# A fused decoder layer on one Trainium2 core: the head's conditioning matmuls set between the transposes of x, first tokens on VectorE, first weight splits at fixed places

## The chip, the cores and the metric

One Trainium2 chip, one of its cores. A core has five engines with instruction queues of their own: TensorE (PE; its weight loads are shown apart as PEld), VectorE (DVE), ScalarE (ACT), GpSimd (POOL) and SyncE (SP, which only issues DMAs here). Sixteen DMA engines are shared by all queues that issue DMAs. The metric is the device time of one execution in microseconds (us); a lower number is better. It covers the program's span and what lies around it.

## The reference

One layer of a hybrid decoder for 256 prompt tokens and 8 x 8 sample tokens (320 columns together), all in float32. What the head of the kernel has to do is the first three lines:

```
mod = silu(c) @ w_ada + b_ada;  sh1, sc1, g1, sh2, sc2, g2 = split(mod, 6)
h = rmsnorm(x, norm1_g) * (1 + sc1) + sh1
p = h @ w_in                      # q, k, v, og, u, ga, gb, alr
o, s_new = gla(q, k, v, decay(alr));  y_a = rmsnorm(o) * silu(og);  y_b = pool(u)
x = x + g1 * ((sigmoid(ga) * y_a + sigmoid(gb) * y_b) @ w_o)
gate, up = split((rmsnorm(x) * (1 + sc2) + sh2) @ w_gu, 2)
y = rmsnorm(x + g2 * ((silu(gate) * up) @ w_down))
```

D_MODEL is 2048 (16 tiles of 128, counted by k), w_in has 11280 columns, w_ada 12288, the FFN 5632.

## The kernel before

Activations stand transposed: 128 features on the partitions, 320 tokens in the free dimension. A projection multiplies in three passes (`mm3`, lines 166 to 168) with both operands split into a high and a low part: of the weights `whi` and `wlo` (ScalarE casts, line 152; VectorE subtracts, line 153), of the tokens `hh` and `hl`. Every weight chunk is loaded by SyncE in program order into the tile `raw`, of which the pool holds three (`bufs=3`); a fourth load waits until the oldest has been split. Tiles `whi` and `wlo` have five buffers each (`WB`).

The head makes the first tokens. It loads c and x, transposes c, makes `scT` = silu(c), and transposes x: 16 tiles, each by three transposes (128, 128 and 64 rows, by `tr`, line 129) into PSUM (`misc`, four buffers) and a copy into `xT` by ScalarE and VectorE in turn (line 458). ScalarE sums the squares of x (line 472); square root, reciprocal and three matmuls with a diagonal matrix `dg` (line 480) give `rx`, the inverse norms, on every partition. `HeadJob` multiplies `scT` with the first two feature tiles' columns of w_ada: four `burst`s of 32 instructions (`ada_mm`, line 218), each on two loads `raw` of w_ada of 512 KB (tag `araw`, eight buffers), then `finish`: a copy `adasb`, a transpose, and `mod` on VectorE (lines 232, 235). `h_unit(k)` makes `hh[k]` and `hl[k]` from `xT[k]`, `rx` and `mod`, on VectorE, GpSimd (64 sample columns) and ScalarE.

Then a loop over slices of k, (0, 2), (2, 4), (4, 8), (8, 12), (12, 16), makes the early projections of each slice and adds them up in SBUF: q, k, v, u, og, ga, gb of the first head and gb of two others. With two feature tiles in a slice, v, og, ga and gb come from one load of 512 columns (`proj_pair`), q, k and u from 256 columns (`proj`). Between these, the bursts and `h_unit`s of the next slice are set; `spill` writes `xT` to DRAM (`xspill`) by GpSimd's queue. Behind the slices follow the other heads' projections, w_o, w_gu and w_down, all in the same manner.

The order on each engine is laid out when the program is built: a scheduler may move an instruction up or down its engine's list, except among those marked by `keep_in_program_order`, which keep theirs (all loads of the slices, and the first matmul of each group in `ada_mm`).

Of the kernel before, what the change touches and what calls it, by code (L numbers as in the profile page):

```python
# [11 lines left out]
F32 = mybir.dt.float32  # L12
F32R = mybir.dt.float32r
I32 = mybir.dt.int32
AF = mybir.ActivationFunctionType
ALU = mybir.AluOpType
# [4 lines left out]
P = 128  # L21
TP, NB, LS = 256, 8, 8
TS = NB * LS
T = TP + TS
D = 2048
KT = D // P
# [10 lines left out]
WB = 5  # L37
AB = 3
SLICES = ((0, 2), (2, 4), (4, 8), (8, 12), (12, 16))
# [41 lines left out]
def body(tc, A):  # L81
    nc = tc.nc
    ctx = ExitStack()
    cp = ctx.enter_context(tc.tile_pool(name="cp", bufs=1))
    wp = ctx.enter_context(tc.tile_pool(name="wp", bufs=3))
# [3 lines left out]
    hp = hcx.enter_context(tc.tile_pool(name="hp", bufs=1, side="right"))  # L89
# [7 lines left out]
    def nm(s):  # L97
        uid[0] += 1
        return "%s_%d" % (s, uid[0])

    def misc():
        return pmisc.tile([P, 512], F32, tag="m", name=nm("pm"))
# [32 lines left out]
    def raw_chunk(src, nk, nn, pool=None, tag="raw", bufs=3):  # L135

        if pool is None and more:
            more.reverse()
            if more[0] is not None:
                pool, bufs = more[0], 2  # L140
        t = (pool or wp).tile([P, nk, nn], F32, tag=tag, bufs=bufs, name=nm("raw"))
        ins = nc.sync.dma_start(t, src)
        if in_order[0]:
            tc.keep_in_program_order(ins)
        return t
# [7 lines left out]
        V.tensor_sub(lo, raw, hi.bitcast(F32))  # L153
        return hi, lo

    def split_chunk(src, nk, nn):

        raw = raw_chunk(src, nk, nn)
        step = 512 // nn
        for k in range(0, nk, step):  # L160
            hi, lo = split(raw[:, k:min(k + step, nk)])
            for j in range(hi.shape[1]):
                yield k + j, hi[:, j], lo[:, j]
# [6 lines left out]
    def proj(w, col, k0, k1, xh, xl):  # L170

        ps = pmain.tile([P, 2, 512], F32, tag="pm", name=nm("ps"))
        for c0 in range(k0, k1, 4):
            nk = min(4, k1 - c0)
            for j, whi, wlo in split_chunk(w[:, c0:c0 + nk, col:col + 256], nk, 256):
                kt = c0 + j
                for i in range(2):
                    mm3(ps[:, i, :T], whi[:, i * P:(i + 1) * P], wlo[:, i * P:(i + 1) * P],
                        xh[kt], xl[kt], kt == k0, kt == k1 - 1)
            ada_pump()  # L180
        return ps
# [14 lines left out]

    def proj_pair(w, col, k0, k1, xh, xl):

        parts = list(split_chunk(w[:, k0:k1, col:col + 512], k1 - k0, 512))
        for half in range(2):  # L200
            ps = pmain.tile([P, 2, 512], F32, tag="pm", name=nm("ps"))
            for j, whi, wlo in parts:
                kt = k0 + j
                for i in range(2):
                    c = (2 * half + i) * P
                    mm3(ps[:, i, :T], whi[:, c:c + P], wlo[:, c:c + P], xh[kt], xl[kt], kt == k0, kt == k1 - 1)
            yield ps
# [78 lines left out]
    def modp(sec, kt):  # L286
        return mod[:, sec * KT + kt, 0:1]

    def mods(sec, kt):
        return mod[:, sec * KT + kt, 1:9].unsqueeze(2).broadcast_to([P, NB, LS])  # L290

    def s3(ap):
        return ap.rearrange("p (b t) -> p b t", t=LS)

    hh = [hp.tile([P, T], F32R, tag="hh%d" % k, name="hh%d" % k) for k in range(KT)]
    hl = [None] * KT
# [70 lines left out]
    def units(h):  # L367
        return [("q", 0, OQ + DK * h), ("k", 0, OK_ + DK * h), ("v", 0, OV + DV * h),
                ("v", 1, OV + DV * h + 256), ("u", 0, OU + 256 * h),
                ("og", 0, OOG + DV * h), ("og", 1, OOG + DV * h + 256),  # L370
                ("ga", 0, OGA + DV * h), ("ga", 1, OGA + DV * h + 256),
                ("gb", 0, OGB + DV * h), ("gb", 1, OGB + DV * h + 256)]


    with tc.tile_pool(name="head", bufs=1) as xp:
# [2 lines left out]
        nc.sync.dma_start(crow[0:1, :], A["c_prompt"])  # L378
        nc.sync.dma_start(crow[1:9, :], A["c_sample"])
        xn = [xp.tile([P, D], F32, name="xn%d" % i) for i in range(3)]  # L380
        x2d = A["x_prompt"][0]
        nc.sync.dma_start(xn[0], x2d[0:P])
        nc.sync.dma_start(xn[1], x2d[P:2 * P])
        nc.sync.dma_start(xn[2][0:TS], A["x_sample"].rearrange("b t d -> (b t) d"))
        V.memset(scT, 0.0)
        make_identity(nc, ident)
        vr0 = xp.tile([6 * KT, P], F32, name="vr0")
# [17 lines left out]
        class HeadJob:  # L405


            def __init__(self, b0, s):
                self.b0, self.s, self.w, self.nk = b0, s, 64 * s, 8 // s
                self.ps = None  # L410
                self.raws = {}
# [34 lines left out]


        xT = []
        for k in range(KT):
            pt = misc()  # L450
            for i in range(3):
                n = P if i < 2 else TS
                tr(pt[:, i * P:i * P + n], xn[i][:n, k * P:(k + 1) * P])
            if k < SLICES[0][1]:
                xT.append(xp.tile([P, T], F32, name="xT%d" % k))
            else:
                xT.append(hp.tile([P, T], F32, tag="hl%d" % k, name="xT%d" % k))
            (S.copy if k % 2 else V.tensor_copy)(xT[k], pt[:, 0:T])

        pt = misc()  # L460
        tr(pt[:, 0:96], vr0)
        tr(pt[:, 96:164], vr1)
# [2 lines left out]
        for sec in (1, 4):  # L465
            V.tensor_scalar(bada[:, sec * KT:(sec + 1) * KT], bada[:, sec * KT:(sec + 1) * KT], 1.0, None, op0=ALU.add)

        ssq = xp.tile([P, 3], F32, name="ssq")
        V.memset(ssq, 1.0)
        for i in range(3):  # L470
            n = P if i < 2 else TS
            S.activation(junk[:n], xn[i][:n], AF.Square, accum_out=ssq[:n, i:i + 1])
        S.activation(ssq, ssq, AF.Sqrt, scale=1.0 / D, bias=epst)
        V.reciprocal(ssq, ssq)
        prs = misc()
# [4 lines left out]
            PE.matmul(prs[:, i * P:i * P + n], lhsT=ones[:n, :], rhs=dg[:n, i, :n], start=True, stop=True)  # L480
        rx = xp.tile([P, T], F32, name="rx")
        V.tensor_copy(rx, prs[:, 0:T])

        def h_unit(k):
            t = xp.tile([P, T], F32, tag="xh", bufs=2, name=nm("xh"))
            V.scalar_tensor_tensor(t[:, 0:TP], xT[k][:, 0:TP], modp(1, k), rx[:, 0:TP], op0=ALU.mult, op1=ALU.mult)
            G.tensor_tensor(t[:, TP:T], xT[k][:, TP:T], rx[:, TP:T], op=ALU.mult)
            G.tensor_tensor(s3(t[:, TP:T]), s3(t[:, TP:T]), mods(1, k), op=ALU.mult)
            G.tensor_tensor(s3(t[:, TP:T]), s3(t[:, TP:T]), mods(0, k), op=ALU.add)
            S.activation(hh[k][:, 0:TP], t[:, 0:TP], AF.Identity, bias=modp(0, k))  # L490
            S.copy(hh[k][:, TP:T], t[:, TP:T])
            hl[k] = hp.tile([P, T], F32R, tag="hl%d" % k, name="hl%d" % k)
            V.scalar_tensor_tensor(hl[k][:, 0:TP], t[:, 0:TP], modp(0, k), hh[k][:, 0:TP].bitcast(F32),
                                   op0=ALU.add, op1=ALU.subtract)
            V.tensor_sub(hl[k][:, TP:T], t[:, TP:T], hh[k][:, TP:T].bitcast(F32))  # L495
# [25 lines left out]
        for h in EARLY_GB:  # L521
            ge = G0()
            ge.gb = merged[h]
            early += [(ge, "gb", i, OGB + DV * h + 256 * i) for i in range(2)]
        for f in HeadJob(0, SLICES[0][1]).steps():
            f()
        for k in range(SLICES[0][1]):
            h_unit(k)
        for si, (k0, k1) in enumerate(SLICES):
            bg = []  # L530
            acc = 0 if si == 0 else 1
# [604 lines left out]
```

## Time and profile before

| what | value |
|---|---|
| median of 3 runs | 2013.61 us (2013.16 to 2013.98) |
| profiled execution, its own time | 2011.32 us |
| span of that execution, first to last instruction | 2009.5 us |
| PE busy | 1956.2 us, 97% of the span |
| VectorE, ScalarE, GpSimd busy | 51%, 41%, 7% |
| mean granted TensorE clock | 0.989 |

Busy shares are of the whole span. The span is shorter than the execution's own time by 1.8 us that lie around it. The profile's times are counted from the first instruction of the program. A PE row's duration is a matmul's latency; matmuls overlap, so the distance between starts is what one costs.

### The profile page before, as it was taken

How to read it: one execution, taken by the hardware profiler on the slowest of the kernel's cores; microseconds unless marked ns; L12 is line 12 of the kernel's file. 1: busy time of each engine (PE TensorE's matmuls, PEld its weight loads, DVE VectorE, ACT ScalarE, POOL GpSimd, SP SyncE). 2: the span in 40 equal slices, each digit the busy share in tenths (PEclk: the TensorE clock that was granted, in tenths of full speed). 3: DMA queues.
4: the chain of work that ended last, by engine and by line, in shares of the span. 5: the costliest groups of instructions: out<-in, count | busy, mean ns of one | idle time of the engine just before them, and what ended most of it. 6: DMA issues, size and time to landing. Idle time of an engine off the chain costs nothing.

```text
span 2009.5 us, 37187 instructions
## 1 busy us (share of the span) xinstructions
PE 1956.2 (97%) x15008; PEld 1848.8 (92%) x15008; DVE 1015.5 (51%) x1881; ACT 820.1 (41%) x1466; POOL 141.8 (7%) x261
## 2 busy tenths in 40 slices
PE   7999999999999999999989999999999999999997
PEld 5789998888899899889979999999999999999997
DVE  3555665465546433665574444444444444444554
ACT  4333374354336333643344333343333344344443
POOL 1112220111001100110020000000000000000000
PEclk9999999999999999999989999999999999999998
DMA  9888754775975887569737666544444544444442
GB/s 301 285 302 272 234 155 147 253 255 186 314 237 167 281 263 229 156 230 340 234 105 223 206 205 203 168 148 154 145 152 149 155 149 147 151 154 144 150 142 91
DMA packets 319598, 400.83 MB, mean 199 GB/s; under 512 B 13529, under 2 KB 259801, under 8 KB 319089
## 3 DMA queue, kind: packets, MB, share of 16 engines
q1 hardware_dynamic: 307154, 358.21, 55.8%
q0 software_dynamic: 12272, 40.25, 5.7%
q8 instruction: 117, 1.92, 0.4%
q14 instruction: 55, 0.45, 0.1%
HBM read 373.96 MB, written 24.67 MB: 198 GB/s over the span
## 4 chain that ended last, share of the span: by engine, by line
PE 91%; DMA 5%; DVE 1%; ACT 1%; issue 1%; SPq 0%; POOL 0%; ACTq 0%; POOLq 0%; DVEq 0%
PE ps L166 27%; PE ps L168 26%; PE ps L167 26%; PE pm L218 5%; DMA raw<-w_in 2%; DMA raw<-w_ada 2%; PE pm L129 2%; PE pm L800 1%; PE pm L769 1%; PE pm L821 1%; DMA xn<-x_sample 1%; DVE wlo L153 0%; PE pm L796 0%; PE pm L758 0%; PE pm L641 0%
## 5 line engine op out<-in xcount | busy, mean ns | idle before, releaser
L153 DVE TENSOR_TENSOR wlo<-raw,whi 128x512 fp32r<-128x512 f32 x952 | 659.6, 697 | 834.0 <-ACT whi L152 827.2
L152 ACT CAST whi<-raw 128x512 fp32r<-128x512 f32 x952 | 587.0, 621 | 1013.4 <-PE ps L167 878.0
L166 PE MATMUL ps<-hh,whi 128*128 128x320 f32 x1408 | 445.9, 317 | 7.3 <-ACT whi L152 3.1
L166 PE MATMUL ps<-h2h,whi 128*128 128x320 f32 x1408 | 437.8, 311 | 5.1 <-ACT h2h L1042 5.1
L168 PE MATMUL ps<-hh,wlo 128*128 128x320 f32 x1408 | 441.6, 314 | 0.2 <-DVE wlo L153 0.2
L167 PE MATMUL ps<-hl,whi 128*128 128x320 f32 x1408 | 440.3, 313 | 0.3 <-DVE hl L495 0.3
L167 PE MATMUL ps<-h2l,whi 128*128 128x320 f32 x1408 | 435.5, 309 | 0.0
L168 PE MATMUL ps<-h2h,wlo 128*128 128x320 f32 x1408 | 435.5, 309 | 0.0
L166 PEld LDWEIGHTS ps<-hh,whi 128*128 128x128 f32 x1408 | 266.6, 189 | 30.8 <-issue 15.8
L168 PEld LDWEIGHTS ps<-hh,wlo 128*128 128x128 f32 x1408 | 266.6, 189 | 8.1 <-issue 6.1
L166 PEld LDWEIGHTS ps<-h2h,whi 128*128 128x128 f32 x1408 | 265.0, 188 | 9.3 <-ACT h2h L1042 6.1
L167 PEld LDWEIGHTS ps<-hl,whi 128*128 128x128 f32 x1408 | 266.9, 190 | 7.0 <-issue 5.4
L167 PEld LDWEIGHTS ps<-h2l,whi 128*128 128x128 f32 x1408 | 264.9, 188 | 0.0
L168 PEld LDWEIGHTS ps<-h2h,wlo 128*128 128x128 f32 x1408 | 264.9, 188 | 0.0
L166 PE MATMUL ps<-ah,whi 128*128 128x320 f32 x704 | 218.7, 311 | 0.0
L168 PE MATMUL ps<-ah,wlo 128*128 128x320 f32 x704 | 217.5, 309 | 0.0
L167 PE MATMUL ps<-al,whi 128*128 128x320 f32 x704 | 217.5, 309 | 0.0
L167 PEld LDWEIGHTS ps<-al,whi 128*128 128x128 f32 x704 | 132.2, 188 | 0.0
L166 PEld LDWEIGHTS ps<-ah,whi 128*128 128x128 f32 x704 | 132.2, 188 | 0.0
L168 PEld LDWEIGHTS ps<-ah,wlo 128*128 128x128 f32 x704 | 132.2, 188 | 0.0
L218 PE MATMUL pm<-raw,scT 128*32 128x128 f32 (+1 forms) x2688 | 109.9, 295 | 8.1 <-DMA raw<-w_ada 8.0
L218 PEld LDWEIGHTS pm<-raw,scT 128*32 128x32 f32 x2688 | 69.1, 111 | 36.0 <-issue 19.5
(279 smaller groups left out, 1542.6 us busy)
## 6 DMA issues: line engine op xcount, KB each, us to landing
raw<-w_ada SPq DMA_DIRECT2D x192, 512.0 KB, 5.8
raw<-w_gu SPq DMA_DIRECT2D x176, 512.0 KB, 3.5
raw<-w_in SPq DMA_DIRECT2D x173, 512.0 KB, 3.9
raw<-w_down SPq DMA_DIRECT2D x80, 512.0 KB, 3.3
S<-state_gla POOLq DMA_DIRECT2D x16, 1024.0 KB, 8.2
o_gs<-S POOLq DMA_DIRECT2D x16, 1024.0 KB, 5.9
raw<-w_o SPq DMA_DIRECT2D x32, 512.0 KB, 4.7
raw<-w_down SPq DMA_DIRECT2D x16, 256.0 KB, 2.6
```

The source lines that it names most:

```text
L129: PE.transpose(out, in_, ident[:k, :k])
L152: S.copy(hi, raw)
L153: V.tensor_sub(lo, raw, hi.bitcast(F32))
L166: PE.matmul(ps, lhsT=whi, rhs=xhi, start=start, stop=False)
L167: PE.matmul(ps, lhsT=whi, rhs=xlo, start=False, stop=False)
L168: PE.matmul(ps, lhsT=wlo, rhs=xhi, start=False, stop=stop)
L218: ins = PE.matmul(ps[32 * j:32 * j + 32, 0:w], lhsT=scT[:, k, :], rhs=raws[j], start=k == 0, stop=k == KT - 1, tile_position=(0, 32 * j))
L769: PE.matmul(pt, lhsT=E["kdn"][:, s, d * P:(d + 1) * P], rhs=E["vn"][:, s], start=s == 0, stop=s == 1)
L800: PE.matmul(pt[32 * j:32 * j + 32, :], lhsT=qeP[:, d, 4 * gg + j, :], rhs=E["S0", gg, d][:, j], start=False, stop=d == 1, tile_position=(0 ...
L821: PE.matmul(pt, lhsT=kpz[:, gg, j, d * P:(d + 1) * P], rhs=E["vp"][:, gg], start=True, stop=True)
```

## The change

Six edits, all in the head:

- The load of the sample rows of x (`xn[2]`) goes from SyncE's queue to ScalarE's, ahead of ScalarE's other work.
- The sum of squares stands ahead of the transposes. Only tiles 0 and 1 of x are transposed at first (copied by VectorE); the rest are made by a function `x_trans`, three tiles after each of the four bursts, and the last four after `finish`'s copy.
- The loads of w_ada of the first job and the first four loads of w_in (q, k, v, u) are issued ahead of everything that needs them.
- `x * rx` of the first two tiles is made early (`xhat`). `h_first` replaces `h_unit` for them and takes GpSimd's share to VectorE.
- The splits of q, k, v and u are five `EarlySplit`s, whose casts and subtractions are marked to keep the order in which the code names them; `split_chunk` hands them out from `ready`.
- `job0` is the `HeadJob` of the first slice, called step by step.

```diff
+        def hi(self):
+            tc.keep_in_program_order(S.copy(self.h, self.raw))
+        def lo(self):
+            tc.keep_in_program_order(V.tensor_sub(self.l, self.raw, self.h.bitcast(F32)))
...
+        nc.scalar.dma_start(xn[2][0:TS], A["x_sample"].rearrange("b t d -> (b t) d"))
...
-        nc.sync.dma_start(xn[2][0:TS], A["x_sample"].rearrange("b t d -> (b t) d"))
...
+        for i in range(3):
+            n = P if i < 2 else TS
+            S.activation(junk[:n], xn[i][:n], AF.Square, accum_out=ssq[:n, i:i + 1])
+        for k in range(SLICES[0][1]):
+            x_trans(k, 0)
...
+        for k in range(SLICES[0][1]):
+            t = xp.tile([P, T], F32, tag="xh", bufs=2, name=nm("xh"))
+            V.tensor_tensor(t, xT[k], rx, op=ALU.mult)
+            xhat.append(t)
+
+        def h_first(k):
+
+            t = xhat[k]
+            S.activation(hh[k][:, 0:TP], t[:, 0:TP], AF.Identity, scale=modp(1, k), bias=modp(0, k))
+            V.tensor_tensor(s3(t[:, TP:T]), s3(t[:, TP:T]), mods(1, k), op=ALU.mult)
+            V.tensor_tensor(s3(t[:, TP:T]), s3(t[:, TP:T]), mods(0, k), op=ALU.add)
+            S.copy(hh[k][:, TP:T], t[:, TP:T])
+            hl[k] = hp.tile([P, T], F32R, tag="hl%d" % k, name="hl%d" % k)
+            V.tensor_scalar(t[:, 0:TP], t[:, 0:TP], modp(1, k), modp(0, k), op0=ALU.mult, op1=ALU.add)
+            V.tensor_sub(hl[k], t, hh[k].bitcast(F32))
...
-        for f in HeadJob(0, SLICES[0][1]).steps():
-            f()
-        for k in range(SLICES[0][1]):
-            h_unit(k)
+        nx = SLICES[0][1]
+        for i, k0 in enumerate(range(0, KT, 4)):
+            job0.burst(k0)
+            while len(xT) < min(nx + 3 * (i + 1), KT - 4):
+                x_trans(len(xT), len(xT) % 2)
+        ew = []
+        for kind, i, col in units(0)[:5]:
+            if kind == "v" and i == 1:
+                continue
+            raw = raw_chunk(win[:, 0:nx, col:col + (512 if kind == "v" else 256)], nx, 512 if kind == "v" else 256)
+            ready[col] = [EarlySplit(raw)] if kind != "v" else [EarlySplit(raw[:, j:j + 1]) for j in range(nx)]
+            ew += ready[col]
+        ew[0].hi()
+        job0.finish()
+        h_first(0)
+        ew[0].lo()
+        ew[1].hi()
+        h_first(1)
+        while len(xT) < KT:
+            x_trans(len(xT), 1)
+        for e in ew[1:]:
+            if e is not ew[1]:
+                e.hi()
+            e.lo()
```

What the scheduler makes of it, at three places. TensorE, where the `rx` matmuls (lines 480 before, 510 after) stand; `pm` on `xn` are transposes of x, `pm` on `raw` is a burst. Before:

```order
L129 MATMUL pm_249<-cst,xn_120 128x128
L129 MATMUL pm_249<-cst,xn_121 128x128
L129 MATMUL pm_249<-cst,xn_122 128x64
L129 MATMUL pm_255<-cst,vr_131 128x96
L480 MATMUL pm_269<-dg,cst 128x128 x2
L480 MATMUL pm_269<-dg,cst 128x64
L218 MATMUL pm_296<-raw_284,scT 32x128 x2
```

After:

```order
L129 MATMUL pm_186<-cst,xn_121 128x128
L129 MATMUL pm_186<-cst,xn_122 128x64
L510 MATMUL pm_201<-dg,cst 128x128 x2
L510 MATMUL pm_201<-dg,cst 128x64
L242 MATMUL pm_220<-raw_159,scT 32x128 x2
```

The `rx` matmuls and all bursts stood behind all 16 tiles of x (`pm_249` is the last of them); now the `rx` matmuls stand behind two tiles (`pm_180`, `pm_186`) and ahead of the first burst, and the other 14 tiles stand behind them.

SyncE, from the last loads of w_ada of the first job on, with what each waits for (DMAHW names are earlier DMAs, PE and DVE the engine that frees a buffer). Before:

```order
L142 DMA raw_436<-w_in 128x2x512 [waits DMAHW7_49]
L142 DMA raw_474<-w_ada 128x4x256 [waits DMAHW0_49,PE_49]
L142 DMA raw_476<-w_ada 128x4x256 [waits DMAHW1_49,PE_49]
L142 DMA raw_479<-w_in 128x2x256 [waits DMAHW5_49,DMAHW2_49,DVE_49]
L142 DMA raw_500<-w_ada 128x4x256 [waits DMAHW3_49,PE_49]
```

After:

```order
L142 DMA raw_345<-w_in 128x2x256 [waits DMAHW5_49]
L142 DMA raw_349<-w_in 128x2x256 [waits DMAHW6_49]
L142 DMA raw_353<-w_in 128x2x512 [waits DMAHW7_49]
L142 DMA raw_359<-w_in 128x2x256 [waits DMAHW0_49,DMAHW5_49,DVE_49,Activation_49]
L142 DMA raw_478<-w_ada 128x4x256 [waits DMAHW1_49,PE_49]
L142 DMA raw_480<-w_ada 128x4x256 [waits DMAHW2_49,PE_49]
```

The load of u (`raw_479`, now `raw_359`), which takes over q's buffer, stood behind two loads of w_ada; now all six loads of w_ada for the next slice stand behind it.

ScalarE, from the copy `adasb` of `finish` to the first tokens (lines 490 and 491 before, 523 and 526 after). Before:

```order
L434 COPY adasb_365<-pm_296 128x128
L152 CAST whi_438<-raw_436 128x512
L152 CAST whi_442<-raw_436 128x512
L490 ACTIVATE hh_90<-xh_372,mod 128x256
L491 CAST hh_90<-xh_372 128x64
```

After:

```order
L458 COPY adasb_364<-pm_220 128x128
L483 COPY xT_343<-pm_339 128x320
L168 CAST whi_347<-raw_345 128x512
L483 COPY xT_391<-pm_387 128x320
L483 COPY xT_397<-pm_393 128x320
L523 ACTIVATE hh_90<-xh_211,mod 128x256
L523 ACTIVATE hh_91<-xh_213,mod 128x256
L483 COPY xT_403<-pm_399 128x320
L483 COPY xT_409<-pm_405 128x320
L526 CAST hh_90<-xh_211 128x64
```

Between `adasb` and the last piece of `hh_90` stood two casts and one activation; now eight instructions, five of them copies of transposed tiles. On VectorE the first subtraction of the weights (`wlo_348`, of q) stands behind `hl` of tile 0; before, it stood ahead of `mod`. From the og projection on, the order is the same on every engine.

## Rows read from the trace of the kernel before

**Rows 1.** The page's chain that ended last, by engine.

```profile
PE 91%; DMA 5%; DVE 1%; ACT 1%; issue 1%; SPq 0%; POOL 0%; ACTq 0%; POOLq 0%; DVEq 0%
```

**Rows 2.** Chain that ended last, 24 to 60 us: start us, us, what.

```profile
31.26 0.28 ACT adasb L434
...
33.55 11.29 DMA raw<-w_in
44.92 0.63 ACT whi L152
...
47.14 0.38 PE ps L166
```

**Rows 3.** PE in order of time: start us, us, operation, count, [idle <-releaser].

```profile
13.44 11.05 PE L129 MATMUL pm<-cst,xn 128*128 128x128 f32 x36 [0.27 <-DVE xT L458]
...
24.63 1.73 PE L480 MATMUL pm<-dg,cst 128*128 128x128 f32 x6
...
29.65 1.52 PE L218 MATMUL pm<-raw,scT 128*32 128x128 f32 x48
31.58 0.33 PE L129 MATMUL pm<-cst,adasb 128*128 128x128 f32 x1 [0.41 <-ACT adasb L434]
34.58 0.68 PE L166 MATMUL ps<-hh,whi 128*128 128x320 f32 x2 [2.68 <-ACT hh L491]
```

**Rows 4.** Stretches: length, busy us (instructions) PE, PEld, DVE, ACT, POOL, clock, DMA, GB/s.

```profile
9.00:12.40 3.40, 1.12 (x4) 0.72 (x4) 0.00 (x0) 2.00 (x2) 0.00 (x0) 1.00 0.95 205
13.00:25.00 12.00, 11.73 (x41) 6.18 (x40) 4.45 (x12) 6.24 (x13) 0.00 (x0) 1.00 1.10 353
...
26.00:28.00 2.00, 2.00 (x35) 1.75 (x38) 0.49 (x1) 0.14 (x1) 0.32 (x1) 1.00 0.07 23
...
26.29:27.99 1.70, 1.70 (x33) 1.58 (x36) 0.49 (x1) 0.00 (x0) 0.32 (x1) 1.00 0.03 10
...
34.90:38.20 3.30, 3.04 (x12) 2.67 (x11) 1.80 (x5) 0.82 (x3) 2.93 (x7) 0.50 1.00 325
38.30:39.90 1.60, 1.60 (x12) 1.60 (x12) 0.00 (x0) 0.34 (x1) 0.00 (x0) 1.00 1.00 304
...
47.00:80.00 33.00, 32.86 (x313) 29.93 (x317) 18.73 (x35) 12.34 (x23) 5.11 (x10) 1.00 0.82 273
```

**Rows 5.** ScalarE in order of time.

```profile
10.18 1.91 ACT L472 ACTIVATE junk<-xn 128x2048 f32<-128x2048 f32 x1 [1.19 <-DMA xn<-x_prompt]
11.99 0.19 ACT L472 ACTIVATION_READ_ACCUMULATOR junk<-xn 128x1 f32 x1
...
15.82 1.28 ACT L473 ACT_TABLE_LOAD   x1
...
22.69 0.43 ACT L458 COPY xT<-pm 128x320 f32<-128x320 f32 x1 [1.40 <-PE pm L129]
...
32.97 0.51 ACT L490 ACTIVATE hh<-xh,mod 128x256 fp32r<-128x256 f32 x1 [0.41 <-DVE xh L486]
34.28 0.24 ACT L491 CAST hh<-xh 128x64 fp32r<-128x64 f32 x1 [0.81 <-POOL xh L489]
```

**Rows 6.** VectorE in order of time.

```profile
17.74 0.64 DVE L479 TENSOR_SCALAR dg<-cst,ssq 128x128 f32<-128x128 f32 x3
...
32.24 0.18 DVE L235 TENSOR_TENSOR mod<-mod,vec 128x18 f32<-128x18 f32 x1
```

**Rows 7.** SyncE's issues in order of time.

```profile
28.24 0.92 SPq L142 DMA_DIRECT2D raw<-w_ada  x2
30.93 0.37 SPq L142 DMA_DIRECT2D raw<-w_in  x1
```

**Rows 8.** DMA issues of 30.93 to 31.30 us: KB each, median us to landing.

```profile
raw<-w_in SPq DMA_DIRECT2D x1, 256.0 KB, 3.2
```

**Rows 9.** PE in order of time, 328 to 333 us.

```profile
328.80 1.14 PE L129 MATMUL pm<-cst,w 128*128 128x128 f32 x9
```

**Rows 10.** PE's waits over the span: us in total, times, longest us.

```profile
PE ps L166 <- ACT whi L152: 3.1, 2, 1.8
```

More of the change, by code (lines that the diff above doesn't have):

```diff
@@ L154, in split, with __init__, split_chunk @@
         return hi, lo
-    def split_chunk(src, nk, nn):
+    ready = {}
+    class EarlySplit:
+        def __init__(self, raw):
+            n = raw.shape[2]
+            self.raw = raw
+            self.h = wp.tile([P, 512 // n, n], F32R, tag="whi", bufs=WB, name=nm("whi"))
+            self.l = wp.tile([P, 512 // n, n], F32R, tag="wlo", bufs=WB, name=nm("wlo"))
+        def hi(self):
+            tc.keep_in_program_order(S.copy(self.h, self.raw))
+        def lo(self):
+            tc.keep_in_program_order(V.tensor_sub(self.l, self.raw, self.h.bitcast(F32)))
+    def split_chunk(src, nk, nn, key=None):
+        if key in ready:
+            k = 0
+            for e in ready.pop(key):
+                for j in range(e.h.shape[1]):
+                    yield k, e.h[:, j], e.l[:, j]
+                    k += 1
+            return
         raw = raw_chunk(src, nk, nn)
@@ L174, in proj @@
             nk = min(4, k1 - c0)
-            for j, whi, wlo in split_chunk(w[:, c0:c0 + nk, col:col + 256], nk, 256):
+            for j, whi, wlo in split_chunk(w[:, c0:c0 + nk, col:col + 256], nk, 256, col if w is win else None):
                 kt = c0 + j
@@ L197, in proj_pair @@
     def proj_pair(w, col, k0, k1, xh, xl):
-        parts = list(split_chunk(w[:, k0:k1, col:col + 512], k1 - k0, 512))
+        parts = list(split_chunk(w[:, k0:k1, col:col + 512], k1 - k0, 512, col))
         for half in range(2):
@@ L448, in body, with x_trans @@
         xT = []
-        for k in range(KT):
+        def x_trans(k, eng):
             pt = misc()
@@ L457, in body @@
                 xT.append(hp.tile([P, T], F32, tag="hl%d" % k, name="xT%d" % k))
-            (S.copy if k % 2 else V.tensor_copy)(xT[k], pt[:, 0:T])
+            (S.copy if eng else V.tensor_copy)(xT[k], pt[:, 0:T])
+        job0 = HeadJob(0, SLICES[0][1])
+        for k0 in range(0, KT, 4):
+            job0.load(k0)
+        ssq = xp.tile([P, 3], F32, name="ssq")
+        V.memset(ssq, 1.0)
+        for i in range(3):
[3 more added lines that the diff above has]
+            x_trans(k, 0)
         pt = misc()
@@ L466, in body @@
             V.tensor_scalar(bada[:, sec * KT:(sec + 1) * KT], bada[:, sec * KT:(sec + 1) * KT], 1.0, None, op0=ALU.add)
[L468 to L472, printed above, removed]
         S.activation(ssq, ssq, AF.Sqrt, scale=1.0 / D, bias=epst)
@@ L482, in body @@
         V.tensor_copy(rx, prs[:, 0:T])
+        xhat = []
+        for k in range(SLICES[0][1]):
[11 more added lines that the diff above has]
+            V.tensor_sub(hl[k], t, hh[k].bitcast(F32))
         def h_unit(k):
```

## The prediction

> **What bounds the kernel now.** I read the page's chain first: 91% of the span is TensorE's [rows 1], so from the point where its stream closes up, whatever is late stays late. Then the stretches, for where that point lies: from 47 to 80 us PE is busy 32.86 of 33 us [rows 4], and over the whole span these projections waited for a cast of their weights only twice, 3.1 us together [rows 10], which is all that could be given back. The change touches only what stands ahead of 47 us, and the order behind is the same. So the question is when the og projection starts, the first whose weights come late. The chain in order of time names its limit: the load of og's weights, issued at 33.55, lands at 44.84; the cast ends at 45.55; VectorE empties a PSUM buffer; PE starts at 47.14 [rows 2]. PE itself began projecting at 34.58 [rows 3] and had q, k, v, u and one burst to do until then: it arrives at 47.1 too. Both limits lie together, so starting PE earlier alone is worth nothing if that load does not come earlier as well.
>
> The load stands last of eight that start at 28.24 (two of w_ada, u, four of w_ada, og) [rows 7], with four writes of xspill among them: 16.6 us to its landing. Ahead of them the DMA engines stood almost still (share 0.07 from 26 to 28 us) [rows 4].
>
> **The clock in the head.** The 36 transposes from 13.44 on take 11.05 us, 0.92 per tile of x [rows 3]; nine transposes later in the kernel take 1.14 us to the last one's end, so some 0.33 a tile [rows 9]. The bursts' first 33 instructions take 1.70 us [rows 4], the 48 behind them 1.52 [rows 3]. The clock column reads 1.00 in that stretch, but by these durations TensorE ran at its lower level, 1.2 GHz, until about 28 us; it rose in the bursts, which followed the `rx` matmuls directly, and never in 11 us of transposes. After the wait for the first tokens it fell again: 0.50 from 34.9 to 38.2 [rows 4].
>
> **The change part by part: when the bursts end.** (1) The sample rows go ahead of the second prompt tile in time. They are 0.5 MB, 1.5 us at 353 GB/s; alone they ran at about 205 [rows 4]. The second prompt tile landed by 10.18 [rows 5]; now at 10.1 (nothing lost) to 11.6 (all of it), and I take 11.0. By the Trainium skill ("Trainium Kernel Development and Optimization", Key Constraints) DMAs of all issuing queues run on the same 16 engines and a second queue saves only the time of issuing; that would put it at 11.6 and the sum 0.6 us higher. The trace agrees only as far as the full share while several loads are under way. The issue itself, ahead of ScalarE's table load, is covered by its wait for c.
>
> (2) The squares: second prompt tile 11.1 to 13.2 (1.91 + 0.19), sample rows to 15.3. Table load, root, reciprocal and the first `dg`, from 15.82 to 17.95 in the rows [rows 5, 6], are 2.13 us: 17.4. Before, this chain ended at much the same time, but PE had transposes to do meanwhile. Now the `rx` matmuls stand ahead of everything but two tiles, so PE stands idle from about 12.5 to 17.4: **5 us of waiting that are new**. The matmuls take 1.73 [rows 3]: 19.1.
>
> (3) From there PE has, ahead of the last burst's end, four bursts and nine tiles. At 1.2 GHz: 4 x 1.70 + 9 x 0.92 + 0.2 for a transpose of vectors = 15.3, so the bursts end at 34.4. Before, they ended just ahead of the copy at 31.26 [rows 2]. The loads of w_ada hide behind this, since the DMA engines had carried them and the first three of w_in by about 26, when they fell still [rows 4]; so do the early xspill writes.
>
> Whether the clock rises in this mix decides most of it. The rows show it rising in real matmuls without a break, and not in transposes; they show no mix. I take the lower level throughout. The Trainium skill ("TensorE: Matmul & The Clock Gate", Part 4: PE-mode transpose) says that the full clock does not engage for transposes. By that rule bursts of 1.7 us between 2.8 us of transposes would stay at 1.2 GHz and the end is 34.4; without it, some us earlier (first rival). The 11 us of transposes agree with it; no row shows bursts among them.
>
> **From the bursts' end (B) to the first released buffer.** PE: one tile 0.9, transpose of `adasb` 0.33 [rows 3]: B + 1.25; then four tiles: B + 2.2, 3.1, 4.0, 4.95. ScalarE, in its new order: copy `xT` to 1.45, cast 0.63 to 2.05, copies of the first two of the four tiles to 2.6 and 3.55, two activations of 0.51 to 4.55, two more copies (0.43 each, the last one's tile ready at 4.95) to 5.4, the cast of 64 columns 0.24 to 5.65 [rows 2, 5]. So the first projection starts at B + 5.7, where it stood 3.3 behind the `adasb` copy's start before. VectorE's own new work (`mod` ends at B + 1.75; four operations on 64 columns at about 0.2, the size of the row on `mod` [rows 6]) is covered by ScalarE's copies; without them it would end at B + 2.6. Then `hl` of 320 columns, bounded by 0.3 and 0.69 and taken as 0.4, and the subtraction of q's weights 0.7: **B + 6.75 = 41.2**.
>
> That is when q's buffer comes free and SyncE goes on. All that follows stands behind u's load: six of w_ada and og. Before, the queue went on at 28.24.
>
> **The load of og.** u lands 3.2 us after its issue [rows 8]; seven loads of 0.52 MB at 353 GB/s [rows 4] are 1.48 each, 10.4: landing at 41.2 + 13.6 + 0.05 = 54.8. Bounds: 12.5 if they run a tenth faster, 16.6 as the same eight ran before. Of the four xspill writes, 0.65 MB or 1.9 us, that stood among them before, none does now, which I count in by taking 13.6. Cast and start, 0.1 + 0.63: og starts at 55.6 instead of 47.14, **8.5 us late**. PE has 60 projections and a burst from 40.1 to 55: 17 us if all ran at the lower level, 10 at the upper; they also wait for u's weights, since its cast now stands ahead of the copy that empties q's PSUM buffer. I add 0.5 for this and for a clock that may be low at og's start (bounds 0 and 3).
>
> **Sum.** 2011.3 (the profiled execution's own time) + 9.0 = 2020.3; it lies 2.3 under the median of the runs, so I expect a median of **2022.6**. Bounds of this case: B from 33.5 to 36, the load from 12.5 to 16.6, the rest 0 to 3: + 6.5 to + 12, 2020.1 to 2025.6.
>
> **Rivals.** *The clock rises early.* The first burst stands directly behind the `rx` matmuls, as it did when the clock rose. Then 19.1 + 1.7 + one tile 0.92 = 21.7; eight tiles at 0.55 (between 0.33 and 0.92) and three bursts at 1.01 (two thirds of the 48's 1.52): B = 29.3, the buffer free at B + 5.8 = 35.1, og at 35.1 + 14.4 = 49.5, 2.3 late. PE would be through with u by 45 and wait 4 us; after the 2.7 us of waiting ahead of 34.58 the clock was at half and 12 matmuls took 3.3 us, about 1.6 lost: + 3.9, 2017.5.
>
> *Not slower: the full clock from the first tile on.* Tiles at 0.33: B = 19.1 + 1.7 + 3.0 + 3.0 + 0.1 = 26.9, the buffer free at 32.5, og at 46.9, 0.2 early: 2013.4. It decides where q's buffer comes free before 32.7 us. For it: nothing but the tiles' rate; against it: 64-row transposes alternate with 128-row ones, which the rows at full clock do not have, and og's load cannot start earlier. Faster by more than 4 us it could only be if the refill were much quicker than any row.
>
> *The delay is given back.* The two later waits for a cast of weights [rows 10] would shrink: 3.1 at most, so 2019.5. Against it: those loads are released by PE's own progress, which shifts with them.
>
> **How the numbers follow.** Within 0.2% (4.0 us) is about what a measurement of this kernel can tell from no change. Forecast, the lower level throughout: 0.62, all slower. Clock rising early: 0.20, half of it above + 4. Full clock from the first tile: 0.13, of it 0.05 faster. Given back, or something else: 0.05, of it 0.02 faster and 0.03 the same. So slower 0.72, same 0.21, faster 0.07. The range runs from 2014.5, which leaves out the third case and a little of the second, to 2026.0.
>
> **What would show it.** Right: PE idle ahead of the `rx` matmuls until about 17.4; tiles between the bursts at about 0.9; first projection near 40; no SyncE issue from about 20 until q's subtraction ends near 41, DMA almost still before it; PE waiting for og's cast near 55. Wrong: tiles under 0.6 between the bursts, u's load issued before 33, or og starting before 47.

## The result

The changed kernel takes 2019.15 us in the median of 14 executions (2016.28 to 2025.36), the kernel before beside it 2012.99 in 14 (2007.39 to 2016.67). The ratio is 1.0036, 95% interval 1.0025 to 1.0046: 7.2 us slower (5.0 to 9.3). The forecast had slower, 2022.6, and a range that holds the median.

The profiled execution took 2024.09 us, with a span of 2022.3 against 2009.5, so its profile shows 12.8 us, nearly twice what the comparison gives; a second profile of the same kernel (below) shows 7.8. In part this is the choice of executions: the profiled one of the kernel before lies 1.7 under its median, that of the change 4.9 over its own. Where the change's two profiles differ is part of the answer.

The profile after, PE in order of time (the columns of [rows 3]):

```profile
6.60 1.84 PE L129 MATMUL pm<-cst,junk 9*128 9x9 f32 x16 [6.60 <-DMA junk<-c_sample]
...
12.02 1.47 PE L129 MATMUL pm<-cst,xn 128*128 128x128 f32 x4 [1.65 <-DMA xn<-x_prompt]
18.46 1.81 PE L510 MATMUL pm<-dg,cst 128*128 128x128 f32 x6 [4.97 <-DVE dg L509]
20.20 1.93 PE L242 MATMUL pm<-raw,scT 128*32 128x128 f32 x32
22.07 2.81 PE L129 MATMUL pm<-cst,xn 128*128 128x128 f32 x9
...
34.89 1.93 PE L242 MATMUL pm<-raw,scT 128*32 128x128 f32 x32
36.75 0.99 PE L129 MATMUL pm<-cst,xn 128*128 128x128 f32 x3
...
37.94 2.42 PE L129 MATMUL pm<-cst,xn 128*128 128x128 f32 x12
...
41.50 1.15 PE L190 MATMUL ps<-hh,whi 128*128 128x320 f32 x2 [1.14 <-ACT hh L526]
...
58.04 0.41 PE L190 MATMUL ps<-hh,whi 128*128 128x320 f32 x1 [4.64 <-ACT whi L152]
```

The new wait ahead of the `rx` matmuls is there (4.97), the three tiles between two bursts take 2.81 and a burst 1.93, both at the lower level of the clock, up to the end of the last burst at 36.75. Only the last four tiles, twelve transposes in 2.42, run at the upper one. The first projection starts at 41.50 against 34.58 [rows 3], and og at 58.04 against 47.14, after a wait of 4.64 that before was not there.

SyncE's issues (a merged row lasts from the first issue to the last one's end, blocked time in it):

```profile
16.64 26.37 SPq L142 DMA_DIRECT2D raw<-w_in  x4
43.12 5.70 SPq L142 DMA_DIRECT2D raw<-w_ada  x6
48.92 1.23 SPq L142 DMA_DIRECT2D raw<-w_in  x1
```

Four loads of w_in take 26.37 us to issue: three are out by 20.2, the fourth, u's, at 42.6, where before the queue went on at 28.24 and u's went out at 30.93 [rows 7]. Behind u stand six loads of w_ada and then og's. The chain that ended last, with start, duration and what, against 33.55, 44.92 and 47.14 of [rows 2]:

```profile
48.92 8.35 DMA raw<-w_in
...
57.37 0.63 ACT whi L152
...
58.04 0.41 PE ps L190
```

The stretches (columns of [rows 4]) from 41.5 to 62 us:

```profile
41.50:45.00 3.50, 3.50 (x12) 3.23 (x13) 3.37 (x6) 1.65 (x4) 0.69 (x1) 0.51 0.33 84
45.00:52.00 7.00, 7.00 (x49) 6.88 (x48) 1.52 (x2) 2.63 (x4) 0.00 (x0) 1.00 1.04 343
53.30:58.00 4.70, 0.09 (x4) 0.00 (x0) 0.09 (x1) 0.64 (x2) 0.00 (x0) 1.00 1.09 372
58.05:62.00 3.95, 3.95 (x16) 3.81 (x17) 1.26 (x2) 1.08 (x3) 0.00 (x0) 0.58 1.04 368
```

While PE waits for og the DMA engines are full (372 GB/s): the load is late because it started late. After the wait the granted clock is low again (0.58 up to 62 us), as it was after the wait for the first tokens (0.51). The two later waits for a cast, 3.1 us together before [rows 10], are still there: PE waited for such casts 7.5 us in three waits from 46 to 104 us, 4.6 of it ahead of og.

### The profile page after: what moved, and what is told of

It is laid out like the page before. It is cut to its first block, busy times and chain, and to the rows that moved or that the text cites. A ratio compares the mean times of both kernels' runs of the same rounds, so it can differ in the third digit from the quotient of the medians.

```text
span 2022.3 us, 37186 instructions
## 1 busy us (share of the span) xinstructions
PE 1960.7 (97%) x15008; PEld 1852.4 (92%) x15008; DVE 1016.4 (50%) x1884; ACT 820.3 (41%) x1467; POOL 137.2 (7%) x255
## 4 chain that ended last, share of the span: by engine, by line
PE 91%; DMA 4%; issue 1%; ACT 1%; DVE 1%; POOL 0%; SPq 0%; ACTq 0%; POOLq 0%; DVEq 0%
PE ps L190 27%; PE ps L192 26%; PE ps L191 26%; PE pm L242 5%; DMA raw<-w_ada 2%; PE pm L129 2%; DMA raw<-w_in 2%; PE pm L867 1%; PE pm L888 1%; PE pm L836 1%; DMA xn<-x_prompt 0%; DMA o_gp<-sf 0%; DVE wlo L153 0%; PE pm L863 0%; PE pm L825 0%
## 5 line engine op out<-in xcount | busy, mean ns | idle before, releaser
L190 PEld LDWEIGHTS ps<-hh,whi 128*128 128x128 f32 x1408 | 267.8, 190 | 33.5 <-issue 14.4
```

Of the source, the lines that this page charges most:

```text
L190: PE.matmul(ps, lhsT=whi, rhs=xhi, start=start, stop=False)
```

## The experiments

Theory: og's start sets the time, its load is held back because SyncE's queue stands at u's load until the subtraction of q's weights has freed a buffer, and that subtraction stands late both by its fixed place in the program and because PE is late (5 us of waiting for `dg`, bursts and tiles at the lower clock). Main rival: PE's lateness alone counts. A profile is of one execution, and two executions of one kernel differ here by up to 5 us in the head, so the ratio gives the size and the profile the mechanism.

| Kernel | Ratio to before (95%) | First projection | Wait ahead of og | og starts |
|---|---|---|---|---|
| before | 1 | 34.58 | none over 0.3 | 47.14 |
| the change, first profile | 1.0036 (1.0025 to 1.0046) | 41.50 | 4.64 | 58.04 |
| the change again | 1.0030 (1.0018 to 1.0042) | 35.61 | 5.32 | 53.04 |
| u's own tile | 1.0014 (1.0003 to 1.0025) | 39.24 | none | 50.83 |
| splits free | 1.0009 (0.9998 to 1.0021) | 37.50 | none | 49.52 |
| rx behind the first burst | 1.0028 (1.0012 to 1.0043) | 33.75 | 5.38 | 51.12 |
| before, with the places alone | 1.0021 (1.0011 to 1.0031) | 35.35 | 6.64 | 54.00 |
| x_sample on SyncE's queue | 1.0020 (1.0008 to 1.0033) | 33.22 | 4.87 | 50.24 |
| bursts in a row | 1.0048 (1.0035 to 1.0061) | 38.80 | 5.43 | 56.25 |
| u's own tile and x_sample | 0.9996 (0.9985 to 1.0008) | 36.02 | none | 46.57 |

**The change again.** No edit.

> The changed kernel again. Theory of the clock (the difference between executions comes from where TensorE's clock rises in the head): in an execution near 2017 the clock rises one step earlier than at 38.2 or does not fall between 41.6 and 45 and between 58.6 and 62, and og starts near 55; in one near 2024 the profile is that of the first. Rival: the head is the same within 1 us in both and the difference lies behind 100 us. Median 1.0025 to 1.0046 of before.

Median 2019.82 (7 executions), ratio 1.0030. The profiled one took 2019.10. PE:

```profile
18.78 1.81 PE L510 MATMUL pm<-dg,cst 128*128 128x128 f32 x6 [4.97 <-DVE dg L509]
20.52 1.93 PE L242 MATMUL pm<-raw,scT 128*32 128x128 f32 x32
22.39 2.12 PE L129 MATMUL pm<-cst,xn 128*128 128x128 f32 x9
...
30.42 1.08 PE L242 MATMUL pm<-raw,scT 128*32 128x128 f32 x32
...
35.61 0.93 PE L190 MATMUL ps<-hh,whi 128*128 128x320 f32 x2 [1.14 <-ACT hh L526]
...
53.04 0.63 PE L190 MATMUL ps<-hh,whi 128*128 128x320 f32 x1 [5.32 <-ACT whi L152]
```

The same wait for `dg`, but the clock rises in the first tiles behind the first burst (2.12 for nine transposes, then bursts of about 1.08): the last burst ends 5.3 us earlier than in the first profile, og starts 5.0 earlier, and the span, 2017.3, is 5.0 shorter. So the theory of the clock held, with og at 53.0 where I had expected it near 55. It also shows something against my reading of the first profile: here PE starts projecting only 1 us later than before, and og still starts 5.9 late, after 5.3 us of waiting. Most of og's lateness does not need PE's.

**u's own tile.**

```diff
+            if kind == "u":
+                raw = junk[:, 0:nx * 256].rearrange("p (k n) -> p k n", n=256)
+                pinned(nc.sync.dma_start(raw, win[:, 0:nx, col:col + 256]))
+            else:
                 raw = raw_chunk(...)
```

> The first raw tile of u lies in the memory of the squares' junk tile instead of taking the buffer of q, so that SyncE's queue no longer stands at u's load until q's subtraction. Theory (the load of og ends last, held up by that place in the queue): SyncE passes u's load by 26, the six loads of w_ada behind it go out as the bursts free their buffers (22 to 33), og's load goes out when q's buffer is free (about 42.6 instead of 48.9) and lands by 51 instead of 57.3; og starts when TensorE is done with u and the next burst (about 53.4) instead of at 58.0, and the time falls by 4 to 6 us, to 1.0008 of before (1.000 to 1.002). Rival (TensorE's late first projection alone sets the time; the load is hidden or the later waits take the difference): no change, 1.0025 to 1.0046.

Ratio 1.0014. SyncE's issues and PE's start of og:

```profile
16.93 3.55 SPq L142 DMA_DIRECT2D raw<-w_in  x3
20.61 0.62 SPq L583 DMA_DIRECT2D junk<-w_in  x1
22.41 10.96 SPq L142 DMA_DIRECT2D raw<-w_ada  x6
40.38 0.37 SPq L142 DMA_DIRECT2D raw<-w_in  x1
```

```profile
39.24 1.15 PE L190 MATMUL ps<-hh,whi 128*128 128x320 f32 x2 [1.15 <-ACT hh L526]
...
49.82 1.08 PE L242 MATMUL pm<-raw,scT 128*32 128x128 f32 x32
50.83 0.41 PE L190 MATMUL ps<-hh,whi 128*128 128x320 f32 x1
```

u goes out at 20.6, w_ada from 22.4 on as the bursts free its buffers, og's load at 40.38, and PE passes from the burst to og without a wait, in an execution whose first projection is 3.6 us later than in the profile above. The wait for og is the hold of SyncE's queue; without it 1.6 to 2.2 parts in a thousand, 3 to 4.5 us, are gone. The rival falls. With the wait gone, PE's own lateness does reach og: the first projection is 4.7 us later than before, og 3.7.

**Splits free.** The two calls that hold the early splits at their places are left out.

```diff
         def hi(self):
-            tc.keep_in_program_order(S.copy(self.h, self.raw))
+            S.copy(self.h, self.raw)
...
-            tc.keep_in_program_order(V.tensor_sub(self.l, self.raw, self.h.bitcast(F32)))
+            V.tensor_sub(self.l, self.raw, self.h.bitcast(F32))
```

> The first splits of w_in are no longer held at their places in the program, so that they stand on ScalarE and VectorE where their data is due. Theory (the places hold the raw buffers, and so SyncE's queue): q's raw buffer is free by 30 instead of 42.6, u's load and the loads of w_ada behind it go out by 34, og's load lands by 47, og starts when TensorE is done with u and the next burst (52.5 to 53.5) instead of at 58.0; time to 1.0008 of before (1.000 to 1.002). Rival (the splits among the transposes' copies delay these, and TensorE with them): the last transposes end later by up to 2 us and the first projection too, 1.002 to 1.005.

Ratio 1.0009. Four loads of w_in now take 13.68 us to issue instead of 26.37, u's going out at 29.97, and PE has no wait ahead of og (49.52):

```profile
16.66 13.68 SPq L142 DMA_DIRECT2D raw<-w_in  x4
```

The same gain by another way, with the loads in the order that the change gives them, so that it is the places and not this order that make the wait. The rival's delay of TensorE isn't seen here (the wait ahead of the first projection grows from 1.14 to 1.42).

**Before, with the places alone.** Bursts, transposes, first tokens and x_sample as before; the splits stand where the change puts them, and the loads of q, k, v and u are all called ahead of the next loads of w_ada, as in the change.

```diff
...
+            raw = raw_chunk(win[:, 0:nx, col:col + (512 if kind == "v" else 256)], nx, 512 if kind == "v" else 256)
...
+        ew[0].hi()
+        steps[-1]()
+        h_unit(0)
+        ew[0].lo()
+        ew[1].hi()
+        h_unit(1)
+        for e in ew[1:]:
...
```

> The kernel before with one part of the change alone: the first splits of w_in at the fixed places of the change (q's cast behind the last burst, q's subtraction behind the first token, the rest behind the second); bursts, transposes, first tokens and the queue of x_sample as before. Theory (the places hold the raw buffers): SyncE stands at u's load until q's subtraction, at about 35 instead of 30.9; og's load goes out at 37.5 to 38 instead of 33.6 and lands near 48.5 instead of 44.8; og starts near 49.5 to 50.5 instead of 47.1, with a wait of 2 to 4 us ahead of it, and the time is 1.001 to 1.002 of before. Rival (the places cost nothing where TensorE is not late): og starts by 48, 0.9995 to 1.0005.

Ratio 1.0021, at the upper edge of what the theory gave. PE and SyncE:

```profile
35.35 0.94 PE L190 MATMUL ps<-hh,whi 128*128 128x320 f32 x2 [2.23 <-ACT hh L515]
...
54.00 0.64 PE L190 MATMUL ps<-hh,whi 128*128 128x320 f32 x1 [6.64 <-ACT whi L152]
```

```profile
17.05 19.55 SPq L142 DMA_DIRECT2D raw<-w_in  x4
36.71 6.99 SPq L142 DMA_DIRECT2D raw<-w_ada  x6
43.80 2.47 SPq L142 DMA_DIRECT2D raw<-w_in  x1
```

VectorE's subtraction of q's weights runs at 35.48, behind the first token's work, and u's load goes out at 36.2 instead of 30.93. PE is 0.8 late at the first projection and 6.9 late at og. The places, with u's load moved ahead of the two loads of w_ada that had gone out at 28.24, cost 4.2 us (2.2 to 6.2); by the middle values that is more than half of what the whole change costs, but the intervals do not fix the share. The 0.8 us by which PE is late is not theirs: the clock rose later in the bursts here, whose first 80 instructions took 4.31 us against 3.22 before.

**rx behind the first burst.** The square root, reciprocal, `dg`, the matmuls for `rx` and the two products become a function that is called behind the first burst and its tiles.

```diff
...
                 x_trans(len(xT), len(xT) % 2)
+            if i == 0:
+                rx_block()
```

> The square root, its reciprocal, dg, the three matmuls that make rx and the products with it stand behind the first burst and its three tiles instead of ahead of the first burst; all else is the change. Theory (5 us of TensorE's wait for dg pass through to the end): the idle stretch from 13.5 to 18.5 is filled with the first burst, which begins when its weights have landed (about 15), the bursts end near 32.5 instead of 36.8, the first projection starts near 37, og near 53.5 to 54 instead of 58.0, and the time falls by 4 to 5 us, to 1.0012 of before (1.0005 to 1.002). Rival (the stretch is hidden, since the transfers of w_ada and w_in set the end of the bursts): the last burst still ends past 35, no change, 1.0025 to 1.0046.

Ratio 1.0028: no difference from the change that this comparison resolves (the 12 executions lie between 2010.91 and 2027.07). PE:

```profile
15.44 1.92 PE L242 MATMUL pm<-raw,scT 128*32 128x128 f32 x28 [0.66 <-DMA raw<-w_ada]
...
23.97 1.93 PE L129 MATMUL pm<-cst,xn 128*128 128x128 f32 x9
...
33.75 0.94 PE L190 MATMUL ps<-hh,whi 128*128 128x320 f32 x2 [1.15 <-ACT hh L527]
```

The 5 us of waiting are gone: the first burst starts 5.1 us earlier than in the second profile of the change. But the clock rises near 24 here and near 23 there, so the work that was drawn forward runs at the lower level, and of the 5.1 us 1.9 arrive at the first projection and at og (51.12). Neither theory fits: the wait isn't hidden, and it doesn't pass through whole.

**x_sample on SyncE's queue.**

```diff
-        nc.scalar.dma_start(xn[2][0:TS], A["x_sample"].rearrange("b t d -> (b t) d"))
...
         nc.sync.dma_start(xn[1], x2d[P:2 * P])
+        nc.sync.dma_start(xn[2][0:TS], A["x_sample"].rearrange("b t d -> (b t) d"))
```

> x_sample goes back to SyncE's queue behind the two prompt tiles; all else is the change. Theory (on ScalarE's queue it runs beside c and the prompt tiles and delays them): c's rows land near 3.8 instead of 6.6 to 7.1, the prompt tiles at 6.9 and 10.1 instead of 9.5 and 12.0, x_sample at 12.4; dg starts at 16.7 to 17.0 instead of 18.0 to 18.4 and the first burst at 18.8 to 19.1. The time falls by about 1.4 us, below what the comparison resolves: 1.002 to 1.0035. Rival (x_sample's place decides nothing, the last of the three tiles lands at the same time either way): dg within 0.3 us of the change.

Ratio 1.0020, which by itself isn't told apart from 1.0030. PE:

```profile
3.78 1.85 PE L129 MATMUL pm<-cst,junk 9*128 9x9 f32 x16 [3.78 <-DMA junk<-c_sample]
...
10.43 0.69 PE L129 MATMUL pm<-cst,xn 128*128 128x128 f32 x2 [2.64 <-DMA xn<-x_prompt]
...
16.86 1.81 PE L510 MATMUL pm<-dg,cst 128*128 128x128 f32 x6 [3.95 <-DVE dg L509]
```

c is there 2.8 us earlier than in the change, the second prompt tile 1.6, and `rx` starts 1.6 earlier. In the change the DMA queues of the first 4 us read (packets, MB, share of 16 engines; q10 carries ScalarE's load, q1 SyncE's):

```profile
q10 hardware_dynamic: 57, 0.47, 47.2%
q1 hardware_dynamic: 10, 0.07, 8.8%
```

The load that was issued first on a queue of its own takes nearly all that is moved until then; c's rows and the prompt tiles stand behind it.

**Bursts in a row.** The ten tiles first, then the four bursts, all else as in the change; once so, and once with u's own tile besides.

```diff
-            job0.burst(k0)
-            while len(xT) < min(nx + 3 * (i + 1), KT - 4):
+            while len(xT) < KT - 4:
                 x_trans(len(xT), len(xT) % 2)
+            job0.burst(k0)
```

> The interleaving undone, all else as in the change: the ten tiles of x come first and the four conditioning bursts in a row behind them. Theory (of the interleaving itself nothing is lost, the splits' places set the time): the bursts run from about 29.5 to 34.5 to 36, the clock rises in them near 33, first projection 38 to 40, q's subtraction ends at 39.5 to 41, and og starts 13 to 14 us behind that with 4 us or more of waiting ahead of it; time 1.002 to 1.0045 of before. Rival (bursts between transposes keep the clock low, and that is what the change loses): the bursts end before 33 and the time is at most 1.0015.

> As the run with the bursts in a row, with u's first raw tile in the squares' memory besides. Theory: no wait ahead of og, which starts about 11.5 us behind the first projection (49.5 to 51.5); 1.0005 to 1.0015 of before. Rival as in that run: at most 1.000.

Ratios 1.0048 and 1.0023 (1.0013 to 1.0033), both a little over what was expected and against 1.0030 to 1.0036 and 1.0014 with the bursts between the tiles. In the first of the two the bursts run from 29.46 (128 instructions in 5.31) and the first projection starts at 38.80. So the interleaving doesn't keep the change slow; both pairs lean the other way, by 2 to 4 us, less than the intervals separate. u's own tile again takes the wait for og away and about 5 us with it.

**Putting edits together.** Three kernels.

> The change with u's first raw tile in the squares' memory and x_sample on SyncE's queue. Theory: dg near 16.9, no wait ahead of og, and og 1.4 us earlier than with u's tile alone at the same rise of the clock: 46.5 to 50; time 0.9995 to 1.0015 of before. Rival (x_sample's place does not reach og): as with u's tile alone, 1.0014.

> Three edits at once on the change: u's first raw tile in the squares' memory, the block of the square root and rx behind the first burst and its tiles, x_sample on SyncE's queue. Theory: no wait ahead of og, the first burst near 15, the bursts' end at 28 to 31 by the clock's rise, first projection 32 to 34.5, og at 45 to 47.5; time 0.999 to 1.0005 of before. Rival (a further transfer binds og): a wait of 2 us or more still stands ahead of og, 1.0005 to 1.002.

> As the run of three edits, with the splits let free instead of a memory of its own for u's first tile. Theory: q's buffer is free by 30, og's load lands by 46, at most 1 us of waiting ahead of og, og at 45.5 to 48, 0.999 to 1.001 of before. Rival (the early splits stand among the transposes' copies and hold up TensorE): the bursts end 1 us or more later than in the run of three edits at the same clock.

u's tile with x_sample on SyncE's queue: 2012.63 us median in 12 executions, ratio 0.9996 (0.9985 to 1.0008), the kernel before within what can be told, and faster than the change. og starts at 46.57, without a wait, though the second prompt tile came 2.5 us later in that execution than in the run with x_sample moved alone. In part that is the draw: the granted clock stayed at 1.00 from 36 to 40 us, behind the wait for the first tokens, where in the profile with u's tile alone it was 0.57 from 39 to 43, which I estimate at 1.7 us (4.00 us at 0.43 below full):

```profile
12.98 0.69 PE L129 MATMUL pm<-cst,xn 128*128 128x128 f32 x2 [4.52 <-DMA xn<-x_prompt]
...
36.02 0.93 PE L190 MATMUL ps<-hh,whi 128*128 128x320 f32 x2 [1.14 <-ACT hh L526]
...
46.57 0.41 PE L190 MATMUL ps<-hh,whi 128*128 128x320 f32 x1
```

The three edits together (rx moved as well) miss: 1.0012 (1.0003 to 1.0020). There is no wait ahead of og and the first burst stands at 14 to 17 us, but in the profiled execution the clock stays low in all four bursts and all tiles, so that the first projection is at 38.27 and og at 51.36. Whether moving `rx` makes this likelier, or it is that execution, stays open.

With the splits free and `rx` moved, 1.0030 (1.0017 to 1.0042): the rival's case, larger than it gave. A tile's copy, on ScalarE and on VectorE, stands behind an early split that waits for its weights, and PE behind the copy:

```profile
25.85 1.23 ACT L168 CAST whi<-raw 128x512 fp32r<-128x512 f32 x2 [9.42 <-DMA raw<-w_in]
26.98 0.42 ACT L483 COPY xT<-pm 128x320 f32<-128x320 f32 x1
```

```profile
26.50 0.69 DVE L171 TENSOR_TENSOR wlo<-raw,whi 128x512 fp32r<-128x512 f32 x1 [8.66 <-ACT whi L168]
27.11 0.48 DVE L483 COPY xT<-pm 128x320 f32<-128x320 f32 x1
```

```profile
27.64 1.84 PE L514 MATMUL pm<-dg,cst 128*128 128x128 f32 x6 [7.45 <-DVE xT L483]
```

**Before, with u and og loaded ahead.**

```diff
...
+            if kind in ("u", "og"):
+                o = 0 if kind == "u" else 512
+                raw = junk[:, o:o + nx * n].rearrange("p (k n) -> p k n", n=n)
+                pinned(nc.sync.dma_start(raw, win[:, 0:nx, col:col + n]))
...
```

> The kernel before with one thing added: the first raw tiles of u and of og lie in the squares' memory, and their loads stand right behind v's, ahead of the next w_ada loads. Theory (in the kernel before too, og's load ends last, since the queue stands still from 20 to 28 for buffers): both tiles land by 30, nothing waits ahead of og, which starts at 45.8 to 46.8 instead of 47.1, and the loads behind are ahead by up to 3 us, so that the two waits near 81 and 88 (3.4 us together) shrink; time 0.9975 to 0.9995 of before. Rival (the loads from 28 to 90 are bound by their bytes alone and TensorE takes up the lead nowhere): the waits near 81 and 88 stay, 0.9995 to 1.0005.

Ratio 1.0005 (0.9996 to 1.0015): the rival holds. Both loads go out by 21.4 and nothing waits ahead of og, but og starts at 48.82, 1.7 us later than before. Of this 0.9 is the clock: the first 80 instructions of the bursts took 4.10 us against 3.22 in the profile before, and PE starts projecting at 35.45. Another 1.0 is the wait for the first token's `hl`, ahead of which u's split now stands:

```profile
35.45 0.56 PE L168 MATMUL ps<-hh,whi 128*128 128x320 f32 x2 [2.68 <-ACT hh L493]
...
37.00 0.63 PE L169 MATMUL ps<-hl,whi 128*128 128x320 f32 x1 [0.99 <-DVE hl L497]
...
48.82 0.41 PE L168 MATMUL ps<-hh,whi 128*128 128x320 f32 x1
```

In the kernel before, PE and that load arrive together, and no gain from an earlier load alone could be measured.

## Why the prediction came out as it did

**The class and the chain were right.** Each step is in the profile: PE idle ahead of `rx`, tiles at about 0.9 between the bursts, SyncE silent from 20.2 to 42.6, the DMA engines still ahead of it, og's cast waited for, and the later waits not shrunk. That og's load is held by q's buffer was shown by taking the hold away in two ways (1.0014, 1.0009) and by putting the places into the kernel before (1.0021). Of the signs that the prediction named, all those for right are in the first profile, 1 to 3 us later than named where they had a time; the second shows one of those for wrong, tiles under 0.6 between the bursts (nine transposes in 1.78).

**The step that failed: "I take the lower level throughout".** It was taken as one case against another (0.62 against 0.20), where it changes from execution to execution. Of nine profiled executions with bursts between the tiles, the clock rose ahead of the last burst's end in seven, at some place between 20.5 and 38 us; in the first profile of the change and in the run of three edits it did not. So the first profile is the forecast's case, and larger than it (12.8 against 9.0), the second is nearer the first rival's and larger than that too (7.8 against 3.9), and the median lies between 3.9 and 9.0. That 2022.6 came within 3.5 us of the median is in part luck: taking one case for all executions made it too high, sums too small in either case made it too low, and the two errors offset each other. The Trainium skill ("TensorE: Matmul & The Clock Gate", Part 4: PE-mode transpose), which I had weighed for a clock that stays low, says that the full clock doesn't engage for transposes; the trace differs: twelve of them took 2.42 us (3.67 in the run of three edits, where the clock stayed low), nine between bursts 1.78 to 2.81, and the clock rose in the mix.

**Terms that were off in size**, by the first profile:

- The second prompt tile: taken at 11.0, at most 11.6, used at 12.02. The Trainium skill's rule ("Trainium Kernel Development and Optimization", Key Constraints), by which a second queue saves only the issue, was the better guide, and even the 11.6 that I worked out from it was too early. I had x_sample take 1.5 us of a shared stream and missed that it also stands ahead of c. So `rx` starts at 18.46 instead of 17.4.
- The bursts' end: 34.4 predicted, 36.75. 1.1 of it is the later start of the first burst (20.20 for 19.1); the rest are bursts of 1.87 from start to start for 1.70, and 0.9 for the transposes of vectors among the second burst, taken at 0.2.
- From there to the first projection 4.75 for 5.7, and to u's load 5.9 for 6.75: the last four tiles ran at the upper clock.
- From u's load to og's landing 13.6: 14.6 in the first profile, 15.5 in the second and 17.0 in the run with the places alone.
- The clock after og's wait, 0.5: the stretch at 0.58 up to 62 us cost about 1.7 (3.95 us at 0.42 below full).
- The upper bound, + 12: it is not the sum of its parts. B at 36 (+ 1.6), the load at 16.6 (+ 3.0) and the rest at 3 (+ 2.5) on top of 9.0 would be + 16.1; the first profile, + 12.8, lies beyond the bound as it was stated.

**Where the loss comes from was weighted wrongly.** The working lays the stress on the 5 us of new waiting. Moved away (rx behind the first burst), they gave nothing that can be measured. The buffer is freed late in the change by two things: PE's lateness, and that the subtraction now stands behind the first token's work, where before it was done 3.7 us ahead of the first projection (30.9 for 34.58) and now 1.1 behind it (42.58 for 41.50, and 36.68 for 35.61 in the second profile). The second was in my sum, but hidden in "from the bursts' end to the first released buffer". Its 4.8 us are in both profiles and stay when PE is on time: they are most of the 5.8 us in the second profile, where PE is 1.0 late, and less than half of the 11.7 in the first, where PE is 6.9 late.

**The rivals.** The early clock: its mechanism occurs, its price of 3.9 was too low, since its buffer came free at 36.75 instead of 35.1 and the loads behind took 15.5 instead of 14.4. Full clock from the first tile: in no profile, and its tile of 0.33 would not have held, since nine transposes at the upper level took 1.78, nearly 0.6 a tile. Delay given back: hardly; where PE waits for og, its later waits for a cast up to 104 us come to 2.4 to 3.6 us besides, against 3.1.

**What stays open.** x_sample's place gave 1 to 1.6 parts in a thousand and, with u's tile, 1.8, where the 1.6 us by which `rx` starts earlier are 0.8; the intervals do not separate these. The first tokens' move from GpSimd to VectorE was not run alone. What decides in which burst the clock rises isn't told by these runs.

## What to carry to other kernels

When a load waits in an in-order queue for a buffer, ask which instruction frees that buffer and what stands ahead of it: an instruction that is fixed behind other work holds not just its own result but every load behind the one that needs its buffer. A price for a wait that is removed or added in the head should be put as a range over where the clock rises, and a single profile shows one draw of it. Two limits that end together, as PE and og's load do in the kernel before, hide the worth of moving either: from an earlier load no gain could be measured, while a later one, by 6.9 us in its profile, cost 4.2 us (2.2 to 6.2).

## What the runs showed of the hardware

- With bursts of 32 small matmuls between nine transposes the granted clock rose anywhere from the tiles at 20.5 us to past 38 us in executions of nearly the same stream; with the bursts in a row (before, and four of the experiments) it rose within them or at their edge each time, as the 128 in 5.31 us show (four bursts of 1.87 would be 7.5).
- A load of 0.5 MB issued 0.4 us ahead on a second queue moved 0.47 MB in the first 4 us while the first queue moved 0.07: the small load of c came 2.8 us later than with both on one queue.
- Transposes of x ran at either level of the clock: nine between two bursts took 2.81 us at the lower and 1.78 at the upper.
